# Releasing weight chunks one by one, with a planned time, in a planner-ordered two-layer decoder trunk

## The chip, the core and the metric

The kernel runs on one core of one Trainium2 chip. TensorE (PE in the profile) does the matrix products, VectorE (DVE) and ScalarE (ACT) the elementwise work, GpSimd (POOL) a few small power operations and two broadcasts, and SyncE (SP) issues nearly all transfers. The metric is the device time of one execution in microseconds; lower is better.

## The reference

Two layers, batch 1, 256 tokens, width 1024, float32. Each layer projects the normalised stream into ten column blocks, runs three groups of attention heads, gates them, and adds an output projection to the stream:

```python
for layer in range(2):
    h = rms_norm(x, norm_g[layer])
    sb_q, sb_k, sb_v, sb_g, mb_q, mb_k, mb_v, mb_g, mem_q, mem_g = split(h @ w_in[layer])   # 1024 x 3584
    o_sb  = stick_breaking_attention(sb_q, sb_k, sb_v) * silu(sb_g)           # 6 heads of 64
    o_mb  = causal_softmax_attention(rotary(mb_q), rotary(mb_k), mb_v) * silu(mb_g)   # 6 heads (one block of 256 keys)
    mk, mv = split(rms_norm(mem, mem_norm_g[layer]) @ w_mem_kv[layer])        # 256 memory tokens
    o_mem = memory_attention(mem_q, mk, mv) * silu(mem_g)                     # 4 heads
    x = x + concat(o_sb, o_mb, o_mem) @ w_out[layer]                          # 1024 x 1024
return rms_norm(x, final_norm_g)
```

Stick-breaking attention weights a key by its sigmoid times the product of one minus the sigmoids of the later keys; it is computed with a softplus and a reverse cumulative sum.

## The kernel before

**Weights.** All weights stream through on-chip memory once. Each column block of a weight (a *piece*: `sb_v`, `mk`, `wo0` and so on) is cut into *chunks* of at most 768 columns, which hold two or three of its eight row blocks `k`. A chunk is loaded into one of `RAW` = 5 buffers `raw`, and split into two reduced-precision halves: `hi_task` copies it to `hi` (on ACT or DVE), and `lo_task` subtracts to get `lo` (always on DVE). There are `LEAD` = 8 buffers each of `hi` and `lo`, so chunk `j` overwrites chunk `j - 8`. When `lo` of a chunk is made, the `raw` buffer is free, and the load five chunks ahead is issued on SP's queue (`dma_chunk`). Every product of the matrices is three matmuls: hi x hi, hi x lo, lo x hi.

**Products.** A piece is used by `N_piece` (the activations stationary, two passes `t` over the tokens, in `nat_unit`), by `T_piece` (the weights stationary, one pass for each 128 columns `c`, in `tr_unit`), by a loop of its own for the very first piece `sb_qk`, or, for the output projection, by `nat_unit` in five stretches: both passes of `wo0` over `k` 0 to 5, the same of `wo1`, then the rest of `wo0`, the rest of `wo1`, and `wo2` whole.

**The order of the instructions.** Nothing is reordered on the chip: each engine runs its instructions in the order in which the program issues them, and waits at each for its semaphores. That order is made when the program is built, by the planner `Sched`. Every stage is a task, a generator that yields requests `R(engines, need=..., alloc=..., cond=...)`. `Sched` keeps a planned clock `T` for each engine, in ns, by its own cost formulas. `S.mark(name)` says that a thing is ready at the planned end of the task's last operation plus `LAT_CROSS` (240 ns); a request with `need` cannot be planned before those times. A `cond`, on the other hand, is only true or false: it carries no time. Of the requests that could start first, the one with the lowest priority number is issued.

`hi_task` is allowed to refill a buffer by such a condition:

```python
e, _ = yield R(*([] if j == 0 else [("act", 0.833 * w)]), ("dve", 0.52 * w), need=[("raw", j)],
               cond=lambda: prog["done"] > j - LEAD)
```

`prog["done"]` is raised by `finish(p)` (lines 480 and 481 of the code before) when the last product of a whole piece has been *issued* by the planner, by the loop of `sb_qk` after each `k`, and once in the middle of `wo0` (lines 995 and 996). From that moment the `hi` copy can be placed on an engine at that engine's own planned clock, whatever the planned time of the product that still reads the buffer; on the chip the semaphore holds the copy until that product has run. `hi_task` and `lo_task` have priority -5 when the chunk is at most `URG` = 2 ahead of the one in use, and 60 otherwise.

**Matmul forms.** Matmuls that use half of the array (scores: form `row`, 64 rows; attention times values: form `col`, 64 columns) are gathered: `_by_form` holds such a request back until as many candidates of its form as its `crowd` (2 unless given) can run, or until `HOLD` = 4000 ns have passed. The requests of this kind are `pair_scores` and `pair_task`, for pairs of heads `c`.

**Names used below.** `a`, `ah`, `al`: softplus of the stick-breaking scores and its halves; `pair_sums` multiplies them with `negT` and `negone` (the cumulative sum). `w`, `wT`: attention weights and their transposes. `ev`, `mxhi`, `mxlo`: the gated head output and its halves, which the output projection reads. `xs`: the residual stream, updated by `resid_task` for each output block and token half; `ss`: its sums of squares; a POOL power makes the norm's factor, then `norm_task` makes `w` on DVE (line 247), PE transposes it (line 226), and ACT and DVE make `Thi` and `Tlo`, the input of the second layer.

Of the kernel before, what the change touches and what calls it, by code (L numbers as in the profile page):

```python
# [17 lines left out]
KT = 8  # L18
# [8 lines left out]
LEAD = 8  # L27
# [163 lines left out]
def hybrid_trunk(ctx: ExitStack, tc: tile.TileContext, x, mem, norm_g, w_in, w_mem_kv, w_out,  # L191
# [5 lines left out]
    S = Sched()  # L197
# [14 lines left out]
    def mm(out, lhsT, rhs, start, stop, **kw):  # L212
        n = _free(rhs)
        half = lhsT.shape[0] == 64 or out.shape[0] == 64
        if lhsT.dtype == FR:
            c = max(60.0, n * 0.4167 + 13.0)
        elif lhsT.dtype == BF:
            c = max(28.0, n * 0.44)
        else:
            c = max(110.0, n * 1.667 + 10.0)  # L220
        nc.tensor.matmul(out, lhsT=lhsT, rhs=rhs, start=start, stop=stop, **kw)  # L221
        m = (lhsT.shape[0], out.shape[0])
        S.op("pe", (0.5 * c if half else c) + pe_mode(m))
# [18 lines left out]
    def tt(out, a, b, op):  # L242
        nc.vector.tensor_tensor(out, a, b, op=op)  # L243
        S.op("dve", 1.0417 * _free(out) + 69.0)
# [9 lines left out]
    def copy(out, in_, eng):  # L254
        if eng == "act":
            act(out, in_)
        else:
            nc.vector.tensor_copy(out, in_)  # L258
            S.op("dve", _free(in_) * (1.0417 if is_psum(in_) else 0.52) + 65.0)

    def R(*eng, **kw):
        kw["eng"] = [e if isinstance(e, tuple) else (e, 0.0) for e in eng]
        return kw
# [70 lines left out]
    for l in range(DEPTH):  # L334
# [4 lines left out]
        for n in names:  # L339
            if n in COLS:  # L340
                c, w = COLS[n]
                order.append(Piece(n, l, wi[:, :, c:c + w], w))
            elif n[:2] == "wo":
                c = 384 * int(n[2])
                w = min(384, D - c)
                order.append(Piece(n, l, wo[:, :, c:c + w], w))
            else:
                c = 256 * (n == "mv")
                order.append(Piece(n, l, wm[:, :, c:c + 256], 256))
    pieces = {(p.name, p.layer): p for p in order}  # L350
    chunks = []
    for p in order:
        i = 0
        while i < KT:
# [6 lines left out]
            for c in range(0, p.width, half):  # L361
                for n, k in enumerate(kk):
                    p.kmap.setdefault(k, []).append((c, len(chunks), n * half))
                chunks.append((p, kk, c, half))
    prog = {"dma": 0, "hi": 0, "lo": 0, "done": 0, "cur": 0}

    def dma_chunk(now=0.0):
        j = prog["dma"]
# [14 lines left out]
    def hi_task():  # L383
        for j, (p, kk, _, w) in enumerate(chunks):
            w = len(kk) * w
            e, _ = yield R(*([] if j == 0 else [("act", 0.833 * w)]), ("dve", 0.52 * w), need=[("raw", j)],
                           cond=lambda: prog["done"] > j - LEAD)
            copy(his[j % LEAD][:, :w], raws[j % RAW][:, :w], e)
            S.mark(("hi", j))
            prog["hi"] = j + 1  # L390
# [55 lines left out]
    def nat_k(p, X, t, acc, k, first, last):  # L446
        w = p.width
        j, o = p.loc(k, 0)
        hi, lo = his[j % LEAD], los[j % LEAD]
        a, b = X[0][:, k, t * 128:(t + 1) * 128], X[1][:, k, t * 128:(t + 1) * 128]  # L450
        mm(acc, a, hi[:, o:o + w], first, False)
        mm(acc, b, hi[:, o:o + w], False, False)
        mm(acc, a, lo[:, o:o + w], False, last)

    def tr_k(p, X, c, acc, k):
        j, o = p.loc(k, c * 128)
        hi, lo = his[j % LEAD], los[j % LEAD]
        mm(acc, hi[:, o:o + 128], X[0][:, k, :], k == 0, False)
        mm(acc, hi[:, o:o + 128], X[1][:, k, :], False, False)
        mm(acc, lo[:, o:o + 128], X[0][:, k, :], False, k == KT - 1)  # L460

    def wneed(p, k, col=0):
        j = p.loc(k, col)[0]
        prog["cur"] = max(prog["cur"], j)
        return [("hi", j), ("lo", j)]

    def nat_unit(p, X, t, acc, xneed, i0=0, i1=KT):

        for i in range(i0, i1):
            k = p.kord[i]  # L470
            yield R("pe", need=wneed(p, k) + xneed(k))
            nat_k(p, X, t, acc, k, i == 0, i == KT - 1)

    def tr_unit(p, X, c, acc, xneed):

        for k in range(KT):
            yield R("pe", need=wneed(p, k, c * 128) + xneed(k))
            tr_k(p, X, c, acc, k)

    def finish(p):  # L480
        prog["done"] = max(prog["done"], max(e[1] for m in p.kmap.values() for e in m) + 1)


    def stat_block(src, sst, i):
# [227 lines left out]
    def pair_task(l, kind, c):  # L712


        vn = VN[kind]
        V = vv[vn]
        k = HCOL[kind] // 128 + c
        _, (o,) = yield R("pe", alloc=["bank"], spare=1, form="col",
                          need=[("wT", l, kind, 2 * c), ("wT", l, kind, 2 * c + 1), (vn, l)])
        w2 = [wTs.pop((l, kind, 2 * c + b)) for b in range(2)]  # L720
        for j in range(2):
            q0 = 0 if j == 0 or kind == "mem" else 128
            for b in range(2):
                mm(o[b * 64:b * 64 + 64, q0:256], V[:, j, 2 * c + b, :], w2[b][:, 256 * j:256 * j + 256 - q0],
                   j == 0, j == 1)
        for wT in w2:
            S.free("wT", wT)
        S.mark(("pv", l, kind, c))
        _, (m,) = yield R("dve", need=[("g", l, k)], alloc=["ev"])
        tt(m, o[:, :256], gT[:, k, :], OP.mult)  # L730
        S.free("bank", o)
        S.mark(("gm", l, k))
        e, _ = yield R(("act", 306.0), ("dve", 200.0))
        copy(mxhi[:, k, :], m, e)
        yield R("dve")
        tt(mxlo[:, k, :], m, mxhi[:, k, :].bitcast(F32), OP.subtract)
        S.free("ev", m)
        S.mark(("mx", l, k))
# [117 lines left out]
    def main():  # L856
# [19 lines left out]
        for l in range(DEPTH):  # L876
            rb = rbx if l == 0 else None
            if l == 0:
                def hneed(k):
                    return [("h", 0, k)]  # L880
# [7 lines left out]
            def bank():  # L888
                _, (acc,) = yield R("pe", alloc=["bank"], spare=0 if "rm" in S.ready else 1)
                return acc  # L890

            def T_piece(n, X, nchunk, need, post):
                p = pieces[n, l]
                for c in range(nchunk):
                    acc = yield from bank()
                    yield from tr_unit(p, X, c, acc[:, :256], need)
                    S.spawn(post(c, acc), 2, S.cur.t)
                finish(p)

            def N_piece(n, X, need, post):  # L900
                p = pieces[n, l]
                for t in range(2):
                    acc = yield from bank()
                    yield from nat_unit(p, X, t, acc[:, :p.width], need)
                    S.spawn(post(t, acc), 2, S.cur.t)
                finish(p)

            def rr_(t, q=False):
                if l == 0:
# [14 lines left out]
            if l == 0:  # L924
                p = pieces["sb_qk", 0]
                accs = []
                for c in range(6):
                    accs.append((yield from bank()))
                for k in range(KT):
                    if k == 0:  # L930
                        j = p.loc(0, 0)[0]
                        for w, h, need in ((his, 0, [("hi", j), ("h", 0, "hi", 0)]), (his, 1, [("h", 0, 0)]),
                                           (los, 0, [("lo", j)])):
                            yield R("pe", need=need)
                            for c in range(3):
                                mm(accs[c][:, :256], w[j][:, c * 128:c * 128 + 128], hT[h][:, 0, :],
                                   w is his and h == 0, False)
                    for c in range(3 * (k == 0), 6):
                        yield R("pe", need=wneed(p, k, c * 128) + hneed(k))
                        tr_k(p, hT, c, accs[c][:, :256], k)  # L940
                    prog["done"] = p.loc(k, 640)[0] + 1
                for c in range(6):
                    S.spawn(evac_T(0, "sb_q" if c < 3 else "sb_k", c % 3, accs[c], 0.125 if c < 3 else 1.0, rbx, "rx"),
                            2, S.cur.t)
                finish(p)
            for i, p in enumerate(ORDER[l]):
                if l == 0 and i == MEM_AT:
                    mem_loads()
# [32 lines left out]
            X = (mxhi, mxlo)  # L981
            hN, mN = mT, hT
            accs = {}
            for i, k0, k1 in ((0, 0, 6), (1, 0, 6), (0, 6, 8), (1, 6, 8), (2, 0, 8)):
                p = pieces[f"wo{i}", l]
                w = p.width
                for t in range(2):
                    if k0 == 0:
                        accs[i, t] = yield from bank()
                    yield from nat_unit(p, X, t, accs[i, t][:, :w], xneed, k0, k1)  # L990
                    if k1 == KT:
                        S.spawn(resid_task(l, i, t, accs[i, t], w, hN), 0, S.cur.t)
                        if l == 1:
                            S.spawn(gain_task(i, t, w), 3 if i == 2 else 70, S.cur.t)
                    elif i == 0 and t == 1:
                        prog["done"] = p.loc(6, 0)[0]
                if k1 == KT:
                    finish(p)
            if l == 0:
                def late_gb():  # L1000
                    yield R("pool", need=[("h", 1, 0), ("h", 1, 1)])
# [55 lines left out]
```

## Time and profile before

| | |
|---|---|
| Median of 3 runs | 297.28 us (297.07 to 298.67) |
| The profiled execution | 297.42 us, of which the span from first to last instruction is 295.6 us |
| Granted TensorE clock, mean | 0.995 |
| PE busy | 284.4 us (96%), 2107 matmuls |
| DVE busy | 229.1 us (78%) |
| ACT busy | 154.0 us (52%) |
| Transfers | 50.05 MB, mean 169 GB/s |

The page gives the busy time of each engine. The view of waits lists who stood idle for whom. The timeline gives, for each row, the start and the length in us, the engine, the line, the operation, its tiles and shape; in square brackets stands how long the engine had been idle before it, and what ended that. Matmuls are pipelined: the time from one start to the next is shorter than the length shown.

### The profile page before, as it was taken

Reading aid. Unit: us, or ns where it says so; the run is one execution under the profiler, and the core shown is the slowest. Engines: PE = TensorE matmul, PEld = TensorE weight load, DVE = VectorE, ACT = ScalarE, POOL = GpSimd, SP = SyncE. Lnnn points to the kernel's source line nnn. Section 1 sums busy time; section 2 is a strip of 40 time slices with the busy share of each in tenths; the row PEclk is TensorE's granted clock in tenths of the full one; section 3 lists DMA queues with packets and bytes.
Section 4 is the critical chain, followed back from the end, with each engine's and each line's share of the span. In section 5 each row is a group of like instructions: output and inputs, shape, how many; then the busy total and the mean of one; then the engine's idle time right before and its main releaser. Section 6 shows DMA issues by size and latency. Waiting matters only on the chain.

```text
span 295.6 us, 5613 instructions
## 1 busy us (share of the span) xinstructions
PE 284.4 (96%) x2107; PEld 269.5 (91%) x2107; DVE 229.1 (78%) x506; ACT 154.0 (52%) x348; POOL 12.4 (4%) x19
## 2 busy tenths in 40 slices
PE   7999999999999999999999997999999999999991
PEld 4999999999999999899899996889999999998991
DVE  4969899997698799984998539774896686799462
ACT  4556879744565559432544114443444665695042
POOL 0311000300000000000120000000000000000001
PEclk9999999999999999999999999999999999999998
DMA  7997957477134873175757465160648136512003
GB/s 237 387 371 237 371 158 222 156 229 231 59 91 146 278 209 117 55 232 161 217 180 265 146 206 156 59 192 26 211 133 238 42 100 170 195 53 92 0 0 142
DMA packets 36795, 50.05 MB, mean 169 GB/s; under 512 B 2337, under 2 KB 34465, under 8 KB 36769
## 3 DMA queue, kind: packets, MB, share of 16 engines
q1 hardware_dynamic: 36192, 48.39, 51.8%
q0 software_dynamic: 288, 1.05, 1.0%
q8 instruction: 16, 0.26, 0.4%
q10 hardware_dynamic: 288, 0.26, 0.3%
q14 instruction: 11, 0.08, 0.1%
HBM read 48.64 MB, written 1.05 MB: 168 GB/s over the span
## 4 chain that ended last, share of the span: by engine, by line
PE 88%; DVE 5%; DMA 2%; issue 2%; ACT 1%; POOLq 0%; POOL 0%; SPq 0%; ACTq 0%
PE bank L221 84%; PE bank L226 4%; DMA raw<-in_w_in_dram 2%; DVE lo L243 2%; DVE hi L258 1%; DVE xs L243 1%; ACT junk L239 0%; DVE a L247 0%; ACT hi L237 0%; ACT xs L239 0%; POOLq L1053 0%; DVE ss L488 0%; DVE w L247 0%; POOL ss L494 0%; DVE Tlo L243 0%
## 5 line engine op out<-in xcount | busy, mean ns | idle before, releaser
L243 DVE TENSOR_TENSOR lo<-raw,hi 128x768 fp32r<-128x768 f32 (+2 forms) x111 | 99.9, 920 | 2.4 <-ACT hi L237 2.3
L221 PE MATMUL bank<-Thi,hi 128*128 128x256 f32 x288 | 83.8, 292 | 0.7 <-DVE hi L258 0.7
L221 PE MATMUL bank<-Tlo,hi 128*128 128x256 f32 x288 | 81.9, 286 | 0.0
L221 PE MATMUL bank<-Thi,lo 128*128 128x256 f32 x288 | 81.8, 286 | 0.0
L237 ACT CAST hi<-raw 128x768 fp32r<-128x768 f32 (+2 forms) x63 | 50.0, 810 | 28.2 <-PE bank L221 13.6
L221 PEld LDWEIGHTS bank<-Thi,hi 128*128 128x128 f32 x288 | 55.9, 195 | 2.9 <-issue 2.6
L221 PEld LDWEIGHTS bank<-Tlo,hi 128*128 128x128 f32 x288 | 55.9, 195 | 0.0
L221 PEld LDWEIGHTS bank<-Thi,lo 128*128 128x128 f32 x288 | 55.9, 195 | 0.0
L221 PE MATMUL bank<-hi,Thi 128*128 128x384 f32 (+1 forms) x160 | 53.9, 337 | 0.0
L221 PE MATMUL bank<-lo,Thi 128*128 128x384 f32 (+1 forms) x160 | 52.0, 325 | 0.0
L221 PE MATMUL bank<-hi,Tlo 128*128 128x384 f32 (+1 forms) x160 | 51.9, 325 | 0.0
L258 DVE CAST hi<-raw 128x768 fp32r<-128x768 f32 (+2 forms) x48 | 26.0, 547 | 22.5 <-PE bank L221 17.4
L221 PE MATMUL bank<-hi,mxhi 128*128 128x384 f32 (+1 forms) x96 | 30.8, 321 | 0.0
L221 PEld LDWEIGHTS bank<-hi,Thi 128*128 128x128 f32 x160 | 30.2, 189 | 0.5 <-issue 0.5
L221 PE MATMUL bank<-lo,mxhi 128*128 128x384 f32 (+1 forms) x96 | 30.5, 317 | 0.0
L221 PE MATMUL bank<-hi,mxlo 128*128 128x384 f32 (+1 forms) x96 | 30.4, 317 | 0.0
L221 PEld LDWEIGHTS bank<-hi,Tlo 128*128 128x128 f32 x160 | 30.2, 189 | 0.0
L221 PEld LDWEIGHTS bank<-lo,Thi 128*128 128x128 f32 x160 | 30.1, 188 | 0.0
L239 ACT ACTIVATE w<-bank,st 128x256 f32<-128x256 f32 (+1 forms) x40 | 17.3, 450 | 11.3 <-DVE st L672 7.4
L221 PEld LDWEIGHTS bank<-hi,mxhi 128*128 128x128 f32 x96 | 18.1, 189 | 0.8 <-issue 0.8
L221 PEld LDWEIGHTS bank<-hi,mxlo 128*128 128x128 f32 x96 | 18.1, 189 | 0.0
L221 PEld LDWEIGHTS bank<-lo,mxhi 128*128 128x128 f32 x96 | 18.1, 189 | 0.0
(114 smaller groups left out, 358.4 us busy)
## 6 DMA issues: line engine op xcount, KB each, us to landing
raw<-in_w_in_dram SPq DMA_DIRECT2D x71, 384.0 KB, 4.2
raw<-in_w_out_dram SPq DMA_DIRECT2D x20, 384.0 KB, 4.4
raw<-in_w_mem_kv_dram SPq DMA_DIRECT2D x8, 384.0 KB, 4.1
uT<-memT_dram SPq DMA_DIRECT2D x8, 256.0 KB, 5.5
xs<-in_x_dram SPq DMA_DIRECT2D x2, 512.0 KB, 6.8
gb<-in_mem_dram SPq DMA_DIRECT2D x2, 512.0 KB, 6.0
raw<-in_w_mem_kv_dram SPq DMA_DIRECT2D x4, 256.0 KB, 4.2
raw<-in_w_in_dram SPq DMA_DIRECT2D x4, 256.0 KB, 3.1
```

Of the source, the lines that this page charges most:

```text
L221: nc.tensor.matmul(out, lhsT=lhsT, rhs=rhs, start=start, stop=stop, **kw)
L226: nc.tensor.transpose(out, in_, idt)
L237: nc.scalar.copy(out, in_)
L239: nc.scalar.activation(out, in_, func, **kw)
L243: nc.vector.tensor_tensor(out, a, b, op=op)
L258: nc.vector.tensor_copy(out, in_)
```

## The change

The three scattered places that raised `prog["done"]` and `finish` go. In their place `release(p, k)` is called after the product that is the last one to use row block `k` of a piece: in the second pass of `nat_unit`, in the last column pass of `tr_unit`, and after each `k` of the `sb_qk` loop. Where `k` is the last row block of a chunk, it marks that chunk as free, with the planned time of that product plus `LAT_CROSS`. `hi_task` now needs the mark of chunk `j - 8`. So a chunk's buffers are released within a piece, and not before their planned time. Besides, `pair_task` of the second pair of memory heads no longer waits for a second candidate (`crowd` 1). The computation and the number of matmuls, copies and loads are the same; which of ACT and DVE makes some copies, and the order on every engine but POOL, differ.

```diff
-    prog = {"dma": 0, "hi": 0, "lo": 0, "done": 0, "cur": 0}
+    prog = {"dma": 0, "hi": 0, "lo": 0, "cur": 0}
...
-            e, _ = yield R(*([] if j == 0 else [("act", 0.833 * w)]), ("dve", 0.52 * w), need=[("raw", j)],
-                           cond=lambda: prog["done"] > j - LEAD)
+            e, _ = yield R(*([] if j == 0 else [("act", 0.833 * w)]), ("dve", 0.52 * w), 
+                           need=[("raw", j)] + ([("free", j - LEAD)] if j >= LEAD else []))
...
+    def release(p, k):
+        for _, j, _ in p.kmap[k]:
+            if chunks[j][1][-1] == k:
+                S.mark(("free", j))
+
     def nat_unit(p, X, t, acc, xneed, i0=0, i1=KT):
         for i in range(i0, i1):
             k = p.kord[i]
             yield R("pe", need=wneed(p, k) + xneed(k))
             nat_k(p, X, t, acc, k, i == 0, i == KT - 1)
+            if t == 1:
+                release(p, k)
-    def tr_unit(p, X, c, acc, xneed):
+    def tr_unit(p, X, c, acc, xneed, last):
         for k in range(KT):
             yield R("pe", need=wneed(p, k, c * 128) + xneed(k))
             tr_k(p, X, c, acc, k)
+            if last:
+                release(p, k)
-    def finish(p):
-        prog["done"] = max(prog["done"], max(e[1] for m in p.kmap.values() for e in m) + 1)
...
-        _, (o,) = yield R("pe", alloc=["bank"], spare=1, form="col",
+        _, (o,) = yield R("pe", alloc=["bank"], spare=1, form="col", crowd=1 if kind == "mem" and c == 1 else 2,
...
-                    prog["done"] = p.loc(k, 640)[0] + 1
+                    release(p, k)
...
-                    elif i == 0 and t == 1:
-                        prog["done"] = p.loc(6, 0)[0]
-                if k1 == KT:
-                    finish(p)
```

More of the change, by code (lines that the diff above doesn't have):

```diff
@@ L895, in T_piece @@
                     acc = yield from bank()
-                    yield from tr_unit(p, X, c, acc[:, :256], need)
+                    yield from tr_unit(p, X, c, acc[:, :256], need, c == nchunk - 1)
                     S.spawn(post(c, acc), 2, S.cur.t)
-                finish(p)
             def N_piece(n, X, need, post):
@@ L905, in N_piece @@
                     S.spawn(post(t, acc), 2, S.cur.t)
-                finish(p)
             def rr_(t, q=False):
@@ L944, in main @@
                             2, S.cur.t)
-                finish(p)
             for i, p in enumerate(ORDER[l]):
@@ L994, in main @@
                             S.spawn(gain_task(i, t, w), 3 if i == 2 else 70, S.cur.t)
-                    elif i == 0 and t == 1:
-                        prog["done"] = p.loc(6, 0)[0]
-                if k1 == KT:
-                    finish(p)
             if l == 0:
```

## The prediction

> **What bounds the kernel now.** I read the page first.
>
> ```profile
> span 295.6 us, 5613 instructions
> ...
> PE 284.4 (96%) x2107; PEld 269.5 (91%) x2107; DVE 229.1 (78%) x506; ACT 154.0 (52%) x348; POOL 12.4 (4%) x19
> ```
>
> PE is busy for 96% of the span. The change leaves every matmul, copy and load in being, so the time can fall only by what PE waits between its products, and rise by new waits and by more switches of form. A busy PE row says little of how fast products follow each other, so I took their rhythm from the chain that ended last (stretch of 384-wide products) and, further below, from neighbouring rows of 256-wide ones.
>
> ```profile
> 213.86 5.21 PE bank L221 x30
> ```
>
> That is 0.17 us for a product of 384 columns; the rows at 146.47 and 146.59 below give 0.12 us for one of 256. Every PE start that comes later than its predecessor plus this rhythm is a wait.
>
> Then the view of waits, for the line that the change is about:
>
> ```profile
> DVE hi L258 <- PE bank L221: 17.4, 9, 4.8
> ```
>
> DVE stands at `hi` copies nine times, 17.4 us in all, for PE to be done with the old chunk. The planner thought the buffer free because the piece's last product had been issued. DVE's waits cost nothing by themselves. They cost where something that PE needs is queued behind them. The timeline shows the worst place, the first cumulative sum of layer 1:
>
> ```profile
> 177.48 1.76 ACT L239 ACTIVATE a<-a 128x384 f32<-128x384 f32 x4
> ...
> 177.71 0.56 DVE L258 CAST hi<-raw 128x768 fp32r<-128x768 f32 x1 [2.27 <-PE bank L221]
> ...
> 180.86 1.82 DVE L243 TENSOR_TENSOR lo<-raw,hi 128x768 fp32r<-128x768 f32 x2
> ...
> 182.02 0.34 PE L221 MATMUL bank<-lo,Thi 128*128 128x384 f32 x1
> 182.60 0.41 DVE L258 COPY sb_k<-bank 128x256 f32<-128x256 f32 x1
> 182.93 1.01 DVE L247 SCALAR_TENSOR_TENSOR a<-bank,a 128x384 f32<-128x384 f32 x2
> 183.86 0.62 DVE L258 CAST ah<-a 128x384 fp32r<-128x384 f32 x2
> 184.26 0.44 PE L221 MATMUL bank<-ah,negT 128*128 128x384 f32 x1 [1.90 <-DVE ah L258]
> ...
> 185.00 0.44 PE L221 MATMUL bank<-al,negT 128*128 128x384 f32 x1 [0.30 <-DVE al L243]
> ```
>
> ACT has the logarithms that DVE's `a` needs at 177.48 + 1.76 = 179.24. DVE is then in a row of four `lo` and two more `hi`, one of which had stood 2.27 us for PE, and comes to `a` at 182.93. PE could start the sums at 182.02 + 0.17 = 182.19; it starts at 184.26, and the first `al` at 185.00 instead of 184.43. That is 2.07 + 0.57 = 2.6 us, the longest wait inside the span.
>
> The second place is the passage from layer 0 to layer 1:
>
> ```profile
> 137.47 0.84 ACT L237 CAST hi<-raw 128x768 fp32r<-128x768 f32 x1 [6.81 <-PE bank L221]
> ...
> 144.25 0.42 DVE L243 TENSOR_TENSOR xs<-bank,xs 128x256 f32<-128x256 f32 x1
> ...
> 146.47 0.28 PE L221 MATMUL bank<-Tlo,hi 128*128 128x256 f32 x1
> 146.59 0.28 PE L221 MATMUL bank<-Thi,lo 128*128 128x256 f32 x1
> 146.66 0.75 DVE L247 SCALAR_TENSOR_TENSOR w<-xs,ss,gb 128x512 f32<-128x512 f32 x1
> ...
> 147.47 0.66 PE L226 MATMUL bank<-cst,w 128*128 128x128 f32 x4 [0.60 <-DVE w L247]
> ...
> 150.36 0.28 PE L221 MATMUL bank<-Thi,lo 128*128 128x256 f32 x1
> ...
> 150.77 0.66 PE L226 MATMUL bank<-cst,w 128*128 128x128 f32 x4
> ```
>
> PE waits 147.47 - 146.59 - 0.12 = 0.76 us for the first `w`, and 150.77 - 150.36 - 0.12 = 0.29 us for the second. Here ACT had stood 6.81 us at a `hi`; the squares and DVE's `lo` behind it were pushed back, and with them the `xs` update at 144.25.
>
> **The change part by part.** The orders of instructions of the two built kernels can be laid side by side; the counts below come from there, the durations from the rows above.
>
> *First sums.* PE runs as many products between the scores and the sums as before (18 of each width). On DVE the order behind the scores was hi, hi, lo, hi, lo, hi, lo, lo, `sb_k`, `a`; it becomes hi, lo, hi, lo, `a`: two `hi`, two `lo` and the `sb_k` copy no longer stand ahead (the copies go to ACT, the `lo` come later). The second `hi` still waits for PE until 177.71, since the product that it waits for stands at the same place. `hi` takes 0.48 and one `lo` 0.87 (half of 1.82, less an overlap), so `a` can start at 177.71 + 0.48 + 0.87 = 179.06; its second half needs 179.24, when DVE is busy anyway. From `a` to the end of the second `al` before: 182.93 to 185.42, 2.5 us. So the last is ready at 181.6, and PE arrives at 182.19. The whole 2.6 us go, with 0.6 to spare. What is moved behind has time: the chunks whose `lo` come later belong to a gate piece that PE reaches only after sb_v. What is late next is the second pair's sums (a rival below). **-2.6 us.**
>
> *Passage.* In the new order DVE makes the four `xs` updates and their sums before the first `lo` of the next layer, not after ACT's blocked `hi`. I walk it: the four end as their products do, about 140.2; three `lo` and one `xs` end 143.05, the next `lo` 143.9. Then comes a 512-wide `hi`, whose load is issued only when the first of those `lo` ends, at 141.2, 1.9 us later than before. The loads of this stretch took:
>
> ```profile
> raw<-in_w_mem_kv_dram SPq DMA_DIRECT2D x2, 384.0 KB, 4.2
> raw<-in_w_mem_kv_dram SPq DMA_DIRECT2D x1, 256.0 KB, 2.9
> ```
>
> This one is of 256 KB: there at 144.1, just in time. `hi`, `lo` and the last `xs` end at 145.8, `w` at 146.5; PE arrives at 146.59 + 0.12 = 146.71, and the 0.76 us go. For the second `w`, ACT now has a 384 KB `hi` ahead of the last square; its load, issued at 142.1, is there at 146.3, the square ends at 147.6, and through the POOL power and two DVE steps `w` ends at about 150.3, when PE has been there since 146.71 + 0.46 + 21 x 0.12 = 149.7: a wait of 0.6 for one of 0.29. Net -0.76 + 0.3: **-0.45 us**, between +0.3 (256 KB also in 4.2) and -1.05 (both waits gone).
>
> The Trainium skill bears on this term: the page "DMA: Bandwidth & Descriptors", section "Anatomy of one DMA — SWDGE (gpsimd) path", gives about 2.0 us plus the bytes over 436 GB/s for a transfer, which would make 2.9 us (an estimate) of the 384 KB load that the row puts at 4.2. By it the second wait vanishes as well and the sum is 0.6 lower. These loads run on the hardware queue beside others, so I keep the row.
>
> *The crowd of the last memory pair, and two split groups.* In layer 1 the new order runs the scores of the two memory pairs in two groups instead of one, and their values products too. What a split costs is read from double and single groups of the same form:
>
> ```profile
> 195.02 1.52 PE L221 MATMUL bank<-wT,sb_v 128*64 128x256 f32 x16
> ...
> 205.70 0.87 PE L221 MATMUL bank<-wT,sb_v 128*64 128x256 f32 x8
> 206.50 0.44 PE L221 MATMUL bank<-hi,Thi 128*128 128x384 f32 x1
> ```
>
> Two singles are 2 x 0.87 = 1.74 against 1.52, and the product behind a group takes 0.44, some 0.1 longer than its fellows (0.34 at 182.02): 0.32 a split. For the scores no single group of the memory form exists, so I take the same, between 0 and twice that. **+0.65 us**, all on PE's path, nothing hides it.
>
> *At nothing.* One load moves ahead of the four `uT` loads on SP, near the end of layer 0; `uT` is read for a piece that comes some 25 us later. POOL's order is the same. Five `hi` copies go from DVE (48 to 43) to ACT, which is busy 52%. The stretch behind the last product is as before. Several stalled `hi` elsewhere (the nine, less the one above) hide behind PE; their going costs and gives nothing. Small waits that a new order opens or closes elsewhere I bound by 0.5 us either way.
>
> The sum: -2.6 - 0.45 + 0.65 = -2.4 us. Against the profiled execution, 297.42 us (span 295.6 and 1.8 around it), that is 295.0; it ran 0.14 above the median of 297.28, so I forecast **294.9 us**.
>
> **The rivals.** *The wait moves to the second sums.* Between first and second sums PE now has 27 products (4.7 us), before 15. In the new order ACT takes two `hi` copies between the steps of the third head and one copy of `ah`; walking it as above, the last `al` is ready 0.3 us before PE. If one of those copies waits for its load, two copies' time (2 x 0.73 us, which I take as the 0.84 row at 137.47 less an overlap of 0.1) is lost less 0.3: 1.2 us, so 296.1. For it speaks the thin margin; against it that the loads were issued more than 4 us before. Chance 0.16.
>
> *The last memory pair comes too late (slower).* From its scores to its transposes PE has 15 products of 256 and 45 of 384 columns, eight transposes and one values group, 11.5 us; DVE has 26 operations in its queue, 10.0 us by rows of their kinds. One is a `hi` whose load is issued when a `lo` of the same queue ends, 4.6 us earlier.
>
> ```profile
> DMA to landing us min/median/max: 2.7/4.1/9.1
> ```
>
> With a median load nothing is lost. From 4.6 us on DVE stands there, and with it the last normalisation. With the longest, 9.1 us, and the 1.5 us of slack already eaten by waits for ACT, PE would stand 4.5 us: 299.3. Against it: the DMA engines are nearly idle so late in the run. Chance 0.07.
>
> *The planned time is not the chip's.* If the planner's clock ran ahead of PE, the `hi` would still stall and hold up what is behind them; then only the cost of the splits is left, 297.28 + 0.65 = 297.9. Against it: ahead of the first sums the order itself has changed, whatever the clock. Chance 0.07.
>
> **How the numbers follow.** The forecast has 0.70. It spans 293.5 (both waits of the passage gone and the splits half as dear: -2.6 - 1.05 + 0.3 = -3.35, and 0.5 for small ones) to 295.7 (the passage at +0.3, small ones at +0.5). The range goes up to 297.3, over the first rival and into the last; the slower rival, half of the last and a little below stay out. A difference of 0.5%, 1.5 us, is about what a measurement of this kernel can tell from none: faster is then the forecast, 0.70; the same is the first and the last rival, 0.23; slower 0.07.
>
> **What would show it.** In the profile after: PE starts the sums of layer 1's first pair without idle time; no DVE `lo` for the gate piece stands between the scores and `a`; the nine `hi` waits of 17.4 us on DVE shrink to less than half, since some `hi` stand at the same products; the first transposes of layer 1 wait under 0.3 us, the second about 0.6; two more groups of half-array matmuls in the last 40 us. The forecast is wrong if PE idles over 1 us at any other place, or if the sums of the first pair still wait for `ah`.

## The result, and the profile after

The changed kernel takes 295.01 us (median of six runs) against 297.06 us before: a ratio of 0.992, with an interval of 0.9895 to 0.9946. In a second group of runs it was 295.3 against 297.6, 0.9906 (0.987 to 0.9942). The profiled execution took 295.21 us, and its page begins:

```profile
span 293.4 us, 5626 instructions
...
PE 284.3 (97%) x2107; PEld 268.9 (92%) x2107; DVE 227.5 (78%) x501; ACT 158.5 (54%) x353; POOL 11.6 (4%) x19
```

PE is busy for as long as before (284.4), and the span is 2.2 us shorter: what went is PE's idle time. The view of waits, for PE alone, shows what is left of it:

```profile
PE bank L221 <- DVE junk L866: 1.2, 1, 1.2
PE bank L221 <- DVE hi L258: 1.0, 1, 1.0
PE bank L226 <- DVE rn L243: 0.4, 1, 0.4
PE bank L226 <- DVE w L247: 0.2, 1, 0.2
```

The first two belong to the start. The waits for `ah` (1.9 us) and `al` (0.3) are gone, the one for `w` has shrunk from 0.6 to 0.2, and a small one for `rn` is new. The first cumulative sum of layer 1, in the timeline of the changed kernel:

```profile
177.74 1.76 ACT L239 ACTIVATE a<-a 128x384 f32<-128x384 f32 x4
177.96 0.56 DVE L258 CAST hi<-raw 128x768 fp32r<-128x768 f32 x1 [1.20 <-PE bank L221]
178.63 0.96 DVE L243 TENSOR_TENSOR lo<-raw,hi 128x768 fp32r<-128x768 f32 x1
179.50 1.01 DVE L247 SCALAR_TENSOR_TENSOR a<-bank,a 128x384 f32<-128x384 f32 x2
...
180.97 1.02 DVE L243 TENSOR_TENSOR al<-a,ah 128x384 fp32r<-128x384 f32 x2
...
182.45 0.34 PE L221 MATMUL bank<-ah,negT 128*128 128x384 f32 x1
```

`a` starts right behind the `lo`, at 179.50, 3.4 us earlier than before; ACT's last logarithm is there at the same moment (177.74 + 1.76 = 179.50). The last `al` ends at 181.99, PE comes at 182.45 and goes through without a stop. The stall of the `hi` at 177.96 is still there: it now stands where DVE had nothing better to do.

The passage from layer 0 to layer 1, PE alone:

```profile
147.40 0.28 PE L221 MATMUL bank<-Thi,lo 128*128 128x256 f32 x1
147.84 0.66 PE L226 MATMUL bank<-cst,w 128*128 128x128 f32 x4 [0.15 <-DVE w L247]
...
150.72 0.28 PE L221 MATMUL bank<-Thi,lo 128*128 128x256 f32 x1
151.03 0.66 PE L226 MATMUL bank<-cst,w 128*128 128x128 f32 x4
```

With the rhythm of 0.12 us, PE waits 147.84 - 147.40 - 0.12 = 0.32 us for the first `w` and 0.19 for the second, 0.5 in all, where it was 0.76 + 0.29 = 1.05.

The scores of layer 1's memory pairs, first in the timeline of before, then in that of the changed kernel:

```profile
255.70 2.00 PE L221 MATMUL bank<-mem_k,mem_q 64*128 64x256 f32 x16
```

```profile
252.84 1.14 PE L221 MATMUL bank<-mem_k,mem_q 64*128 64x256 f32 x8
...
257.33 1.13 PE L221 MATMUL bank<-mem_k,mem_q 64*128 64x256 f32 x8
```

That is 2.27 us for 2.00; the values products, split in the same way, take 1.08 twice for 1.95. With 0.1 for the product behind each extra group the two splits cost 0.68 us.

### The profile page after: what moved, and what is told of

The parts are those of the page before. It is cut to its first block, busy times and chain, and to the rows that moved or that the text cites. A ratio compares the mean times of both kernels' runs of the same rounds, so it can differ in the third digit from the quotient of the medians.

```text
span 293.4 us, 5626 instructions
## 1 busy us (share of the span) xinstructions
PE 284.3 (97%) x2107; PEld 268.9 (92%) x2107; DVE 227.5 (78%) x501; ACT 158.5 (54%) x353; POOL 11.6 (4%) x19
## 3 DMA queue, kind: packets, MB, share of 16 engines
q1 hardware_dynamic: 36192, 48.39, 52.8%
q0 software_dynamic: 288, 1.05, 1.1%
HBM read 48.64 MB, written 1.05 MB: 169 GB/s over the span
## 4 chain that ended last, share of the span: by engine, by line
PE 87%; DVE 5%; DMA 4%; issue 1%; ACT 1%; POOLq 0%; POOL 0%; SPq 0%; DVEq 0%; ACTq 0%
PE bank L221 82%; PE bank L226 4%; DMA raw<-in_w_in_dram 3%; DVE lo L243 2%; DMA raw<-in_w_mem_kv_dram 1%; DVE hi L258 1%; DVE xs L243 1%; DVE rn L243 0%; ACT xs L239 0%; POOLq L1053 0%; DVE w L247 0%; DVE mxlo L243 0%; DVE ev L243 0%; POOL ss L501 0%; ACT rn L239 0%
## 5 line engine op out<-in xcount | busy, mean ns | idle before, releaser
L237 ACT CAST hi<-raw 128x768 fp32r<-128x768 f32 (+2 forms) x68 | 54.1, 807 | 21.2 <-PE bank L221 13.8
L258 DVE CAST hi<-raw 128x768 fp32r<-128x768 f32 (+2 forms) x43 | 23.6, 548 | 20.9 <-PE bank L221 15.7
L239 ACT ACTIVATE junk<-xs 128x384 bf16<-128x384 f32 (+2 forms) x16 | 8.4, 524 | 23.5 <-DVE xs L243 18.4
L679 DVE TENSOR_REDUCE st<-bank 128x1 f32<-128x256 f32 (+1 forms) x40 | 13.2, 372 | 6.8 <-PE bank L221 6.8
```

The source lines that it names most:

```text
L237: nc.scalar.copy(out, in_)
L239: nc.scalar.activation(out, in_, func, **kw)
L679: nc.vector.tensor_reduce(st[:, t:t + 1], sc[:, r0:r1], axis=AX.X, op=OP.max, negate=True)
```

## The experiments

In the table each ratio is to the kernel before, run in the same group. "Stall" is the sum of the times that DVE and ACT stood at a `hi` copy until PE was done with the buffer, from the view of waits of each profiled execution (before: 17.4 + 13.6 = 31.0 us; in E3 the view names none of ACT).

| kernel | median us | ratio (interval) | stall us |
|---|---|---|---|
| changed kernel | 295.01 | 0.992 (0.9895 to 0.9946) | 29.5 |
| changed kernel, again (E5) | 295.30 | 0.9906 (0.987 to 0.9942) | 25.9 |
| E1 before, two chunks held back | 293.88 | 0.9875 (0.9834 to 0.9917) | 31.3 |
| E2 by chunk, no time | 305.11 | 1.0247 (1.0196 to 1.0298) | 52.8 |
| E3 by piece, with time | 293.51 | 0.9871 (0.9832 to 0.9909) | 9.5 |
| E4 no second edit | 296.58 | 0.9972 (0.9948 to 0.9997) | 27.6 |
| E6 three DVE operations more | 296.38 | 0.9939 (0.9909 to 0.9969) | 28.3 |
| E7 by chunk, 1 us early | 294.92 | 0.9893 (0.9852 to 0.9933) | 42.0 |
| E9 by chunk, 0.3 us late | 294.46 | 0.9882 (0.9857 to 0.9906) | 24.7 |
| E8 by chunk, 0.6 us late | 293.09 | 0.9836 (0.9794 to 0.9878) | 27.1 |
| E10 by chunk, 1 us late | 294.24 | 0.9864 (0.9834 to 0.9894) | 26.5 |
| E11 by chunk, 2 us late | 293.09 | 0.9834 (0.9809 to 0.9858) | 12.0 |
| E12 by piece, 0.6 us late | 293.37 | 0.9851 (0.9826 to 0.9875) | 14.0 |

### E1: the order at one place, and nothing else

```diff
 (the kernel before)
         stt(a, z, 0.0, a, OP.max, OP.add)
+        S.mark(("a", l, h))
 ...
-            e, _ = yield R(*([] if j == 0 else [("act", 0.833 * w)]), ("dve", 0.52 * w), need=[("raw", j)],
+            e, _ = yield R(*([] if j == 0 else [("act", 0.833 * w)]), ("dve", 0.52 * w), need=[("raw", j)] + [("a", 1, 1)] * (j == 76),
```

> The kernel before, with one edit: the hi copy of the third gate chunk of layer 1 (and with it the two lo and the hi that follow it) must wait until the step a of the second head of layer 1 has been issued; the untimed release stays as it was. In the new order DVE has two lo and the sb_k copy between the last stalled hi and a, where there were four lo, two hi and the sb_k copy; PE runs the same 36 products ahead of the first sums; nothing is split at the memory pairs. Theory A (the gain is the order at this one place): a starts at about 178.2 + 2 x 0.87 + 0.4 = 180.3 instead of 182.9, the wait of 2.6 us at the first sums of layer 1 shrinks to 0 to 0.6, the time is 294.7 to 295.3. Theory B (the gain needs the planned times through the whole kernel): 296.7 to 297.3.

Measured: 293.88 us, 0.9875: more than theory A asked for. Its timeline:

```profile
177.66 0.56 DVE L258 CAST hi<-raw 128x768 fp32r<-128x768 f32 x1 [2.27 <-PE bank L221]
178.13 1.82 DVE L243 TENSOR_TENSOR lo<-raw,hi 128x768 fp32r<-128x768 f32 x2
...
180.20 1.01 DVE L247 SCALAR_TENSOR_TENSOR a<-bank,a 128x384 f32<-128x384 f32 x2
...
182.14 0.34 PE L221 MATMUL bank<-ah,negT 128*128 128x384 f32 x1
```

`a` starts at 180.20 (expected 180.3), PE begins the sums at 182.14 instead of 184.26. The stalls sum to what they were, 31.3 us against 31.0, the 2.27 us one included; what stands behind that one has changed. So the gain does not come from stalling less. It is the order at this place (behind it some products of layer 1 change places too). From the start of the first scores of layer 0 to that of the last product its profile takes 254.6 us, that of before 257.2: the 2.6 us that were walked. The rest of the 3.0 us between the two profiled executions (294.41 and 297.42) lies ahead of that, where both have the same instructions (see E7 to E12). Without the two split groups, its ratio lies below that of the whole change, though the intervals overlap.

### E2 and E3: by chunk without the time, by piece with it

```diff
 (E2: the changed kernel)
-                S.mark(("free", j))
+                S.ready["free", j] = 0.0
 (E3: the kernel before; done(n) stands at the three places of prog["done"], and hi_task needs the mark as in the change)
+    def done(n):
+        for j in range(prog["done"], n):
+            S.mark(("free", j))
+        prog["done"] = max(prog["done"], n)
```

> The changed kernel, but each chunk is released with time zero, so that the planner takes its buffer for free as soon as the last product has been issued in the plan: the release is chunk by chunk and untimed. Theory A (the planned time makes the order): DVE's order ahead of a is again hi, lo, hi, lo, hi, lo, hi, lo, sb_k, and the first sums of layer 1 wait about 1.9 us; 296.3 to 298. Rival (the finer release itself brings the gain, since copies no longer stall for a whole piece): 294.5 to 295.5.

> The kernel before, but what is released there (a whole piece, at the same three places) is marked with the planner's time of the last product, and the hi copy needs that mark; no crowd edit. Theory A (the planned time makes the order): a of the first sums of layer 1 follows on DVE after the lo of the value piece and the sb_k copy, no gate lo is ahead of it, and the 2.6 us at the first sums go; the late release of whole pieces may cost up to 1 us elsewhere: 294.5 to 296. Rival (the finer release brings the gain): nothing gained, 297 or more.

E2 took 305.11 us, far beyond the 298 that I had allowed; E3 took 293.51, below its range. PE's waits in E2, those over 0.5 us behind the start:

```profile
PE bank L226 <- DVE w L247: 2.1, 2, 1.9
PE bank L226 <- DVE rn L243: 2.0, 3, 1.0
PE bank L221 <- DVE ah L258: 1.6, 1, 1.6
PE bank L221 <- DVE sb_v L258: 1.4, 1, 1.4
```

The wait for `ah` is back (1.6 us; I had walked 1.9), and three others of its kind stand beside it: transposes that wait for `w` and `rn`, values products that wait for `sb_v`. The queue ahead of `a` is the one that was expected; the other three I did not follow step by step, but the stalls at `hi` have grown from 31.0 to 52.8 us. In E3 this view has no PE wait left but those at the start (its timeline has two short ones besides, 0.29 and 0.39 us at the memory pairs of layer 0):

```profile
PE bank L221 <- DVE junk L864: 1.2, 1, 1.2
PE bank L221 <- DVE hi L258: 0.8, 2, 0.5
PE bank L221 <- DVE lo L243: 0.5, 1, 0.5
```

So of the two parts of the first edit, the time is the one that brings the gain; the finer release without it loses 2.5%. That this is because the planner puts still more copies ahead of their buffers fits the longer stalls, but was followed only at `a`. With the time, whole pieces come out 0.4 to 0.5% below single chunks, but the intervals overlap. Counted in the same way, E3's profile takes 253.8 us, that of the changed kernel 255.2. Of these 1.4 us the traces show 1.1: the two split groups (0.68) and the waits at the passage (0.5) and at the rope of layer 0 (0.59, see below), which E3 does not have, less its own 0.29 and 0.39.

### E4: without the second edit

```diff
-        _, (o,) = yield R("pe", alloc=["bank"], spare=1, form="col", crowd=1 if kind == "mem" and c == 1 else 2,
+        _, (o,) = yield R("pe", alloc=["bank"], spare=1, form="col",
```

> The changed kernel without its second edit (the last memory pair may again be held for company). The orders differ only near the end: in layer 1 the values products of the last pair come 21 products of 384 columns later, and right behind them stands a product that needs their result. Theory A (the edit is what keeps the last pair off PE's path): PE waits there for three DVE steps, 0.42 + 0.30 + 0.42 and their hand-overs, 1.5 to 1.8 us; 296.5 to 296.8. Rival (the edit does nothing for the time): 294.8 to 295.2.

Measured: 296.58 us. Near its end:

```profile
275.45 0.34 PE L221 MATMUL bank<-lo,mxhi 128*128 128x384 f32 x1
275.71 1.08 PE L221 MATMUL bank<-wT,mv 128*64 128x256 f32 x8
...
277.65 0.44 PE L221 MATMUL bank<-hi,mxhi 128*128 128x384 f32 x1 [0.86 <-DVE mxhi L258]
278.11 0.45 PE L221 MATMUL bank<-hi,mxlo 128*128 128x384 f32 x1
```

The product behind the values group starts 277.65 - 275.45 = 2.20 us after the one ahead of it; in the changed kernel, at the group that starts at 272.69, the same stretch takes 1.28. With 0.29 more at the `mxlo`, 1.2 us are lost: theory A's wait, somewhat shorter than it said. The edit is what keeps the last pair off PE's path here. (The profiled execution, 295.80 us, is one of the short ones of E4: it lacks the 0.59 us that the changed kernel's profile loses at the rope of layer 0.) On the kernel before, the same edit alone leaves the order of every engine as it is: it acts only where the pairs come apart.

### E6 (beside E5): how much room there is

```diff
 (the changed kernel, ahead of the step a; the scratch tile dum and a GpSimd memset of it are left out here)
+        if l == 1 and h == 0:
+            for _ in range(3):
+                nc.vector.tensor_tensor(dum, dum, dum, op=OP.subtract)
```

> The changed kernel as it is, beside the other three of this group: 294.7 to 295.4 by every theory.

> The changed kernel with three more DVE operations (128x512, a scratch tile that nothing reads) put right ahead of the step a of layer 1's first head, of which the planner knows nothing, so that no order moves. Estimated from the 128x512 and 128x768 operations of the trace at 0.6 us each, 1.8 us. Theory A (DVE's queue ahead of a sets the start of the first sums, with 0.46 us to spare in the trace of the changed kernel, from the end of the last al at 181.99 to the start of the sums at 182.45): PE waits 1.3 us there, and the time is 296.0 to 296.6. Rival (the waits of DVE at the hi copies behind a give the time back): under 0.5 us, 295.0 to 295.5.

```profile
179.73 2.14 DVE L647 TENSOR_TENSOR dum<-dum 128x512 f32<-128x512 f32 x3
...
183.12 0.44 PE L221 MATMUL bank<-ah,negT 128*128 128x384 f32 x1 [0.28 <-DVE ah L258]
183.86 0.45 PE L221 MATMUL bank<-al,negT 128*128 128x384 f32 x1 [0.29 <-DVE al L243]
```

E5 took 295.30 us, as expected. In E6 the three operations took 2.14 us and moved `a` 2.06 us back (it started at 181.79). PE, whose product ahead of the sums starts at 182.50, waits 0.45 us at `ah` and 0.57 at `al`, 1.0 in all; the time rose by 296.38 - 295.30 = 1.1 us. PE did not get it back later, as the rival had it. The room is then about 1 us (2.06 less 1.0), not 0.46: I had asked for the last `al` at the start of the sums, but they take `ah`, `al`, `ah`, `al` in turn, so that the last one is needed three products later.

### E7 to E12: the planned time moved

```diff
 (E7, E9, E8, E10, E11: x = -1000, 300, 600, 1000, 2000 ns; E12: E3 with x = 600)
-                S.mark(("free", j))
+                S.ready["free", j] = S.cur.t + LAT_CROSS + x
```

> The changed kernel, but each chunk's planned time of release is 1 us earlier than the planner's time of the product. Theory A (the order is only as good as the planned time): DVE's order ahead of a is as in the untimed one, the first sums of layer 1 wait 1 to 2 us again, and the time lies between the changed kernel's 295 and the untimed one's 305: 296.5 to 300. Rival (any time near the product does, and the untimed one was slow for another reason): 294.3 to 295.5.

> The changed kernel, but each chunk's planned time of release is 0.6 us later than the planner's time of the product. In the new order the scores and the values products of layer 1's two memory pairs stand together again. Theory A (what the changed kernel still loses to the one with whole pieces and times is mainly the two split groups, 0.69 us by its trace): 294.0 to 294.6. Rival (the finer release costs in other places): 294.8 to 295.5.

> The changed kernel with each chunk's planned time of release 0.3 us later. Layer 1's memory scores stand in one group, its values products in two. Theory A (a small margin on the planned time is what helps: with 0.6 us the waits at the passage and at the rope transposes went too): between the changed kernel and the one with 0.6 us, 293.3 to 295.0. Theory B (each shift shakes the orders anew, and what comes out is chance within some us): anything from 293 to 297, and no line through the shifts.

> The same with 1.0 us later. Scores and values of layer 1's memory pairs stand in one group each; in layer 0 the values products of the first form stand in three groups instead of two. Theory A (margin helps until buffers come too late): 292.9 to 293.8. Theory B (chance of the orders): anything from 293 to 297.

> The same with 2.0 us later. A chunk's hi copy is planned 2 us after its buffer is free; a lo and the next load follow it. Theory A (margin helps until buffers come too late): above the one with 1 us, 293.5 to 295.5, with PE waits at weight products that the others don't have. Theory B (chance of the orders): anything from 293 to 297 without such waits.

> The kernel before with its whole pieces released at the planner's time of their last product plus 0.6 us. Theory A (margin helps here too, where nine-tenths of the stalls are gone already): 292.8 to 293.6, the waits of 0.29 and 0.39 us at the memory pairs of layer 0 gone. Theory B (chance of the orders): anything from 293 to 297.

E7 fell against theory A: 294.92 us, like the changed kernel. Its timeline shows why the first sums do not mind 1 us:

```profile
180.12 1.01 DVE L247 SCALAR_TENSOR_TENSOR a<-bank,a 128x384 f32<-128x384 f32 x2
...
182.27 0.34 PE L221 MATMUL bank<-ah,negT 128*128 128x384 f32 x1
```

One `hi` and the `sb_k` copy came ahead of `a`, which starts at 180.12 instead of 179.50. That is inside the room. What was lost in E2 needs an error larger than 1 us.

E9 and E12 lie where theory A had them (294.46 and 293.37 us; in E12 the waits at layer 0's memory pairs are gone, as it had said). E8, at 293.09, is faster than either of its theories allowed; both memory groups are whole again, as expected. E10, at 294.24, lies above its theory A. E11 is as fast as E8 and behind the start has none of the waits at weight products that theory A had foreseen, with stalls of only 12.0 us. So "margin helps until buffers come too late" did not hold up to 2 us; late release costs nothing there. Nor do the ratios of the six shifts lie on a line (from 1 us early to 2 us late: 0.9893, 0.992 and 0.9906, 0.9882, 0.9836, 0.9864, 0.9834).

Part of these differences has nothing to do with the orders. Up to the first scores of layer 0, PE, DVE, ACT and SP have the same instructions in the same order in every kernel here, and yet the scores start at different times. The row of E10, then that of E11:

```profile
32.72 0.49 PE L221 MATMUL bank<-sb_q,sb_k 64*128 64x256 f32 x2
```

```profile
30.97 2.23 PE L221 MATMUL bank<-sb_q,sb_k 64*128 64x256 f32 x24
```

From there to the start of the last product the profiles take 255.2 us (the changed kernel, both times), 254.8 (E7), 253.9 (E9) and 253.4 (E8, E10 and E11 alike). The 1.5 us between the spans of E10 and E11 (292.8 and 291.3) are thus the start's; how the executions without a profile started, no run shows. Behind the start, E8 has both memory groups whole again, and no wait over 0.2 us at the passage or the rope; E9 has one of the groups split; E10 has a wait of 0.29 us at the passage. A margin that helps up to 0.6 us and changes nothing beyond fits these profiles, one for each kernel. So does the luck of each order: E7, with its time 1 us early, has both groups whole too. It stays open. What is settled: the eight kernels with a planned time that keep the last memory pair off PE's path (the changed kernel, E3 and E7 to E12), and E1, are faster than before. The two with the lowest ratios, E8 and E11 at 0.9836 and 0.9834, come out below the changed kernel too; E8's interval just touches that of E5.

## Why the prediction was right, and where it was not

Forecast 294.9 us, measured 295.01 and, again, 295.30. That the first came within 0.1 us is partly luck: between the two profiles there are three terms that the sum did not have, 0.59 us at the rope, 0.24 at the start and -0.35 at the third sums, and the passage came out 0.1 lower. One bound was added up wrongly: the passage at +0.3 and small waits at +0.5 make 297.28 - 2.6 + 0.3 + 0.65 + 0.5 = 296.1, not 295.7; the range reached beyond both. Step by step:

*The first sums* (-2.6 us). Right, with its mechanism. PE's start, `a`'s start (179.06 forecast, 179.50 measured) and the room (0.6 forecast, 0.46 by the same count) came as walked, and E1 shows that this order alone is the gain. One thing was left out: the third sums of layer 1, whose eight products took 0.35 us longer before than other groups of their kind, lost that too.

*The passage* (-0.45). Right in sum: 0.5 us of waits for 1.05, and 0.17 + 0.53 = 0.7 in the second profile of the same kernel. Its parts came out otherwise: the first wait did not vanish. The term that was mis-sized is one load. In the changed kernel's timeline, and for the first of the two copies in that of E5:

```profile
142.14 0.37 SPq L314 DMA_DIRECT2D raw<-in_w_mem_kv_dram  x1
143.10 6.83 SPq L314 DMA_DIRECT2D raw<-in_w_in_dram  x6
...
145.49 0.43 DVE L258 CAST hi<-raw 128x512 fp32r<-128x512 f32 x1 [0.50 <-PE bank L221]
...
147.13 0.83 ACT L237 CAST hi<-raw 128x768 fp32r<-128x768 f32 x1 [2.53 <-PE bank L221]
```

```profile
145.22 0.43 DVE L258 CAST hi<-raw 128x512 fp32r<-128x512 f32 x1 [0.35 <-DMA raw<-in_w_mem_kv_dram]
```

The 256 KB load that I had taken as 2.9 us, "just in time", kept DVE's 512-wide `hi` waiting until 145.49 - 142.14 = 3.35 us after its issue. The row of the changed kernel names PE as what ended the wait, that of E5 the load; the view of transfers has the load at 3.3 us from issue to landing, and at 3.1 in E5, and in both the copy starts 0.1 us later. With PE 0.8 us later than in the profile of before when it gets here, every other step of the walk came within 0.2 us: `hi`, `lo` and `xs` took 1.6, and the wait of 0.3 is this load's excess of 0.45 less the 0.2 that the walk had to spare. ACT's 384 KB `hi`, whose row names PE too, started 147.13 - 143.10 = 4.0 us after the issue of its load, and 4.2 in E5, which is when the load landed in both: the row's 4.2. The Trainium skill's page "DMA: Bandwidth & Descriptors", section "Anatomy of one DMA — SWDGE (gpsimd) path", is on transfers that GpSimd issues, and would make 2.9 us of this load, which SP issues (an estimate); neither trace agrees. The second wait is smaller than forecast in the first profile, where PE itself comes later by the first; in E5 it is 0.53, near the 0.6 that were forecast.

*Two split groups* (+0.65). Right: 0.68. But the cause was not worked out. I put the splits beside the second edit; they come from the order that these planned times make (E4 splits them as well, while in E7, E8, E10 and E11, with other times, they are whole), and that edit, which I priced at nothing, saves 1.2 us where they are split.

*Small waits elsewhere* (0, within 0.5). Right only in part. In the profile of the changed kernel the rope of layer 0 has a new one:

```profile
72.68 0.34 PE L221 MATMUL bank<-lo,Thi 128*128 128x384 f32 x1
...
73.44 0.52 PE L226 MATMUL bank<-cst,rn 128*128 128x128 f32 x3 [0.42 <-DVE rn L243]
```

PE waits 73.44 - 72.68 - 0.17 = 0.59 us for `rn`, on whose engine, DVE, a `hi` had stood 0.48 us for its load at 68.96; in the second profile of the same kernel it is 0.28, and in E4 and E6, whose order is the same up to there, 0 and 0.06. So this wait goes with one load, from execution to execution. I had looked at the order of layer 1 and the passage, not at that of layer 0, where the sums, values products and transposes also stand in another order. Against it stand the 0.35 of the third sums. What is left between the 2.4 us forecast and the 2.05 and 2.3 measured is inside the intervals.

*The signs.* Two of them were wrong though the forecast was not. I said that the nine stalls of 17.4 us on DVE would shrink to less than half:

```profile
DVE hi L258 <- PE bank L221: 15.7, 9, 4.8
```

They did not. A planner that knows the wait still places the copy on an engine with nothing else to do; ahead of the first sums the stall was then free. And I said that no `lo` of the gate piece would stand ahead of `a`; of its four, two do, as my own walk had it (hi, lo, hi, lo, a). The two waits of the passage, "under 0.3" and "about 0.6", came at 0.32 and 0.19, and in the second profile at 0.17 and 0.53.

*The rivals.* The second sums were not late: no wait for them in PE's view. The last memory pair was not late, but E4 shows that its place is real: 3.6 us later in the order and PE waits 1.2. The planner's clock is close enough to the chip's: a shift by 1 us either way changes little, while leaving the time out (E2) costs 7.8 us against the kernel before.

## What to carry to other kernels

When a planner writes the order of in-order queues, give each buffer's release a planned time; a rough one will do: here anything from 1 us early to 2 us late was 0.8 to 1.7% faster than before, while release by order alone was worse by chunk (305.1 us) than by piece (297.3). Don't count stalls, look for what stands behind them: kernels with 9.5, 31 and 42 us of stalled copies lay within 0.5% of each other, and the order of one short queue ahead of `a` held nearly the whole gain. A local edit at one wait that was walked through in the timeline (E1) gave as much as the general mechanism, and showed where that one's gain comes from.

## What the runs showed of the hardware that I had not expected

The start varies by more than most terms of the sum. In profiles of kernels with the same instructions up to there, the first weight product began at 4.80 us (E3), 5.06 (before), 5.30 and 5.00 (the changed kernel, twice) and 6.46 (E10), each time waiting for the first copies and their loads. The rhythm behind it differs too. In the changed kernel products of 256 columns start 0.21 us apart until 8.85 us, and 0.12 apart from then on; in E3 and E8 most are 0.12 apart from the first. At the first scores of layer 0 this makes 30.97 (E11) to 32.72 us (E10). E1 and the kernel before, which first differ in the middle of layer 1, are at 31.29 and 31.71. A single profile says little below 2 us unless its parts are compared one by one, or counted from a common point behind the start; and waits behind a load, such as those of the passage (0.5 and 0.7 us) and the rope (0.59 and 0.28), move by some tenths between two profiles of the same kernel.
